# Saving matmuls by sevens in four more blocks, and one weight sum of each seven made by an accumulating transfer

## The chip, the cores and the metric

The kernel runs on 1 core of one Trainium2 chip. The metric is device time of one execution in microseconds (us). Of the kernel before there are three timed runs, with a median of 2232.99 us (2231.83 to 2235.12). Engines are called as in the profile: PE (TensorE, matmuls; PEld loads its weights), DVE (VectorE), ACT (ScalarE), POOL (GpSimd), SP (SyncE, which issues nearly all transfers).

## The reference, cut to what matters

Two layers on 256 tokens of width 2048. Each layer is a mixer (gated delta rule and gated linear recurrence in layer 0; two kinds of attention in layer 1) and then a SwiGLU feed-forward of inner width 5632; at the end stands an RMS norm over rows.

```python
h = h + mixer(rmsnorm(h, norm), ...)                 # w_in, w_out and the mixing between
h = h + swiglu(rmsnorm(h, ffn_norm[layer]), ffn_w_gate[layer], ffn_w_up[layer], ffn_w_down[layer])
...
def swiglu(hn, w_gate, w_up, w_down):
    return (jax.nn.silu(hn @ w_gate) * (hn @ w_up)) @ w_down
```

All is float32. The change touches the feed-forward, the first projection of the kernel and the last norm.

## The kernel before, in words

**A float32 product as three matmuls.** Every weight tile `raw` (128 x 1024 float32, 512 KB) is loaded by SP (L173 in `load`), rounded by ACT into a high half `whi` (L179) and subtracted by DVE into a low half `wlo` (L180). PE then adds x_high·w_high, x_high·w_low and x_low·w_high into a PSUM bank. In the feed-forward these are L404, L405 and L406 in `Bank.add`, with 512 columns each.

**Buffers.** `raw` has 3 buffers, and the feed-forward has 4 more (`raw4`): of each 7 loads 4 go to `raw4` and 3 to `raw`. `whi` has 4 buffers, `wlo` 3, `thi` and `tlo` 2 each. SP issues its loads in one order, each when a buffer is free.

**Blocks.** `ffn` (L482) walks over 11 pieces of the inner width, in three rounds of 4, 4 and 3. A round first makes each of its pieces with one block of gate and up weights (`in_gu`), and then has two down blocks (`in_dn`, p = 0 and 1), for two times 512 columns each. A `block` (L409) holds four result banks `F[t][i]`, for token half t and result i.

**Sevens.** A group m of four weight tiles (two rows of tiles by two results) costs 8 products with two token halves, 48 matmuls. Where m is in `comb`, `seven` (L424) does it by seven products, as in Winograd's form of Strassen's rule, 42 matmuls. It needs sums of weight tiles, made by `total` (L372): DVE adds (L375), ACT rounds (L378, `thi`), DVE subtracts (L379, `tlo`). The sums, of four tiles b11, b12, b22 and b21, are T1 = b11 + b12, T3 = b12 + b22, T2 = T1 + b22, T4 = T2 + b21 (the signs lie on the token side). It also needs sums of the token side, made by `combine` (L382 to L393) once for four tiles of x. The products go to four more banks M0 to M3, which `ends` (L449) folds into `e` tiles: one copy by ACT (L451) and four adds by DVE (L453). Gate and up blocks have two groups by sevens (the first has none), down blocks have one. The steps of the sevens are spread between the plain units of the block (L476); `hooks` places side work at a plain unit, such as `turn` (L487: transposes of the gated result through banks `Ph`) and `late` (L504: `combine` for the down blocks).

**Order.** The instructions of each engine are put in order when the kernel is built, by a scheduler with estimated costs; semaphores then hold them to their data. At the end of the second feed-forward the order of DVE and ACT is written by hand (`second_half`, L1137).

**Start and end.** `first` (L210) makes four projections from 16 tiles of x and weights, loaded as four single tiles and then pairs (L219); high and low halves are made tile by tile for the first two pairs and then pair by pair (L227). After each four tiles ACT squares them (L250). At the end, the row norm is taken from partial sums of squares `ssp` (L317); `root` (L1142) makes two small DVE steps (L1145) and a square root on ACT (L1147), `rate` inverts it (L1151 to L1153), `ready` scales and stores (L1157, L1159, L1161).

Of the kernel before, what the change touches and what calls it, by code (L numbers as in the profile page):

```python
# [5 lines left out]
AF = mybir.ActivationFunctionType  # L6
# [4 lines left out]
D = 2048  # L11
# [36 lines left out]
def body(tc, A, out):  # L48
# [161 lines left out]
    def first(src, n, w):  # L210

        m = T + n * 128
        xw = [h.rearrange("p a b -> p (a b)")] + [ogp.tile([128, 4 * D // 2], F32, name=f"xw{i}", tag="og") for i in range(3)]
        xw = [t[:, 0:4 * m].rearrange("p (k n) -> p k n", n=m) for t in xw]
        Ps = [acc.tile([128, T], F32, name="Pw", tag="acc") for _ in range(n)]
        for a, b in [(k, k + 1) for k in range(4)] + [(k, k + 2) for k in range(4, NK, 2)]:  # L219
            nc.sync.dma_start(xw[a // 4][:, a % 4:a % 4 + b - a], src[:, a:b])  # L220
            if b == 12:
                nc.sync.dma_start(tab[:, 0:NTAB0], A["tab"][:, 0:NTAB0])
                nc.sync.dma_start(col[:, 16:], A["col"][:, 16:])
        for u in range(NK // 2):
            hi = wh.tile([128, 1024], F32R, name="whi")
            lo = wl.tile([128, 1024], F32R, name="wlo")
            for a, b in [(0, 1), (1, 2)] if u < 2 else [(0, 2)]:  # L227
                ks = range(2 * u + a, 2 * u + b)
                for k in ks:
                    x = xw[k // 4][:, k % 4, 0:T]  # L230
                    S.activation(X[:, k, 0], x, AF.Copy, scale=w[:, k:k + 1])
                    V.scalar_tensor_tensor(out=X[:, k, 1], in0=x, scalar=w[:, k:k + 1], in1=X[:, k, 0].bitcast(F32),
                                           op0=ALU.mult, op1=ALU.subtract)
                raw = xw[u // 2][:, u % 2 * 2 + a:u % 2 * 2 + b, T:]
                c = slice(512 * a, 512 * b)
                rows = lambda t: t[:, c].rearrange("p (k n) -> p k n", n=n * 128)
                if u == a == 0:
                    V.tensor_copy(rows(hi), raw)
                else:
                    S.copy(rows(hi), raw)  # L240
                V.tensor_sub(rows(lo), raw, rows(hi).bitcast(F32))
                for k in ks:
                    for i, P in enumerate(Ps):
                        ws = slice((k % 2 * n + i) * 128, (k % 2 * n + i + 1) * 128)
                        PE.matmul(P, hi[:, ws], X[:, k, 0], start=k == 0, stop=False)
                        PE.matmul(P, hi[:, ws], X[:, k, 1], start=False, stop=False)
                        PE.matmul(P, lo[:, ws], X[:, k, 0], start=False, stop=k == NK - 1)
            if u % 2:
                sq = xw[u // 2][:, :, 0:T]
                tc.keep_in_program_order(S.activation(sq, sq, AF.Square))  # L250
        return Ps, [t[:, :, 0:T] for t in xw]
# [60 lines left out]

    def sumsq(g, *ts):
        for t in ts or range(2):
            j = (mx.tile([128, 1024], F32, name="junk", tag="T", bufs=3)[:, 0:512] if more else
                 mx.tile([128, 512], F32, name="junk", tag="t2", bufs=4))
            S.activation(j, h[:, t, g * 512:(g + 1) * 512], AF.Square, accum_out=ssp[:, t, g:g + 1])  # L317

# [50 lines left out]
        return f  # L369


    def total(a, b, name):  # L372

        t = mx.tile([128, 1024], F32, name=name, tag="T", bufs=3)
        V.tensor_tensor(out=t, in0=a, in1=b, op=ALU.add)  # L375
        hi = fp.tile([128, 1024], F32R, name="thi", tag="thi", bufs=2)
        lo = fp.tile([128, 1024], F32R, name="tlo", tag="tlo", bufs=2)
        S.copy(hi, t)  # L378
        V.tensor_sub(lo, t, hi.bitcast(F32))  # L379
        return t, (hi, lo)  # L380

    def combine(x4):  # L382

        f = mx.tile([128, 4, T], F32, name="cf", tag="T", bufs=3)
        c = mx.tile([128, 4, 2, 128], F32, name="cc4", tag="T", bufs=3)
        r = fp.tile([128, 2, 4, 2, 128], F32R, name="comb", tag="comb", bufs=3)
        V.tensor_tensor(out=f, in0=x4[:, :, 0].bitcast(F32), in1=x4[:, :, 1].bitcast(F32), op=ALU.add)
        a11, a21, a12, a22 = (f[:, 2 * j:2 * j + 2, t * 128:(t + 1) * 128] for j in range(2) for t in range(2))
        for i, (x, y) in enumerate(((a21, a22), (a21, a11), (a22, c[:, 1]), (a12, c[:, 2]))):
            V.tensor_tensor(out=c[:, i], in0=x, in1=y, op=ALU.subtract)  # L390
        S.copy(r[:, 0], c)
        V.tensor_tensor(out=r[:, 1], in0=c, in1=r[:, 0].bitcast(F32), op=ALU.subtract)
        return r  # L393

    class Bank:
# [3 lines left out]
        def add(self, A, B):  # L399

            hi, lo = (t.rearrange("p (k n) -> p k n", n=512) for t in B)
            for kk in range(2):
                xh, xl = A(kk)
                PE.matmul(self.t, xh, hi[:, kk], start=self.i == kk == 0, stop=False)  # L404
                PE.matmul(self.t, xh, lo[:, kk], start=False, stop=False)  # L405
                PE.matmul(self.t, xl, hi[:, kk], start=False, stop=kk == 1 and self.i == self.n - 1)  # L406
            self.i += 1

    def block(src, x, comb, nd, hooks, tail=0, lead=2, trail=None):  # L409

# [13 lines left out]
        def seven(m):  # L424
# [16 lines left out]
            M[2].add(cx(2), w)  # L441
            yield
            b21 = load(src(0, 2 * m + 1))
            F[0][0].add(q(1, 0), split(b21))
            yield
            F[1][0].add(q(1, 1), total(t, b21, "T4")[1])
            yield

        def ends():  # L449
            c1, v, w5, w7 = (mx.tile([128, 512], F32, name=f"e{i}", tag=f"e{i}", bufs=1) for i in range(4))  # L450
            S.copy(c1, M[0].t)  # L451
            for o, a, b, op in ((v, M[2], c1, ALU.subtract), (w5, M[1], v, ALU.add), (v, M[3], v, ALU.add), (w7, M[3], w5, ALU.add)):
                V.tensor_tensor(out=o, in0=a.t, in1=b, op=op)  # L453
# [28 lines left out]
    def ffn(L, then, fin=None):  # L482
# [18 lines left out]
        for groups in ((0, 2, 2, 2), (2, 2, 2, 2), (2, 2, 2)):  # L501
# [3 lines left out]
            for j in range(piece):  # L505
# [8 lines left out]
                a = [fp.tile([128, 512], F32, name=f"fa{t}", tag="fa", bufs=2) for t in range(2)]  # L514
                for t in range(2):
                    if e:
                        V.tensor_tensor(out=a[t], in0=F[t][0], in1=e[t][0], op=(ALU.add, ALU.subtract)[t])
                    S.activation(a[t], a[t] if e else F[t][0], AF.Silu, scale=nrm["rs"][:, t:t + 1])
                for t in range(2):
                    if e:  # L520
                        V.tensor_tensor(out=e[t][1], in0=F[t][1], in1=e[t][1], op=ALU.add)
                    V.scalar_tensor_tensor(out=a[t], in0=e[t][1] if e else F[t][1], scalar=nrm["rs"][:, t:t + 1], in1=a[t],
                                           op0=ALU.mult, op1=ALU.mult)
                    todo.append((hid, j, t, a[t]))
                b += 1
            u0 = 2 * (b - piece)
            for p in range(2):
                end = b == NB and p == 1
                hooks = {2: turn} if todo else {}
                if p == 0 and piece == 4:  # L530
                    hooks.update(late)
                if end and fin:
                    hooks.update({5: lambda: then(0), 6: lambda: then(1)})
                last = (3, 1, 3) if end and fin else (0, 5 if 4 in hooks else 2)
                F, e = block(lambda i, u: dn[2 * p + i, u0 + u], lambda k: hid[:, k], {0: lambda: ch[0]}, piece, hooks, *last)
                hs = [[h[:, t, (2 * p + i) * 512:(2 * p + i + 1) * 512] for i in range(2)] for t in range(2)]
                for t in range(2):
                    for i in range(2):
# [598 lines left out]
    def second_half(add):  # L1137

        o = fo[0]
        x, y, z = ([f[:, t:t + 1] for t in range(2)] for f in (xf, yf, zf))  # L1140

        def root(t):  # L1142

            for i, o in ((2, z[t]), (3, x[t])):
                V.scalar_tensor_tensor(out=o, in0=ssp[:, t, i:i + 1], scalar=1.0 / D, in1=part[:, t:t + 1] if i == 2 else z[t],  # L1145
                                       op0=ALU.mult, op1=ALU.add)
            S.activation(y[t], ssp[:, t, 3:4], AF.Sqrt, scale=1.0 / D, bias=z[t])  # L1147

        def rate(t):
# [15 lines left out]
        add(0, 1)  # L1165
        sumsq(3, 0)
        add(1, 0)
        root(0)
        sumsq(2, 1)
# [107 lines left out]
```

## Time and profile before

| | |
|---|---|
| median of 3 runs | 2232.99 us |
| the profiled execution | 2232.51 us, of which its span is 2230.7 us |
| granted PE clock | 0.999 |
| instructions on PE / DVE / ACT / POOL | 11026 / 2716 / 1670 / 6 |
| weights and other data moved | 422.29 MB, mean 189 GB/s |
| feed-forward of layer 0 and of layer 1 | about 424 to 1152 us and 1526 to 2221 us of the span |

A line of the page's list of groups gives source line, engine, operation, result and inputs, how many, then busy time and mean duration of one; behind the second bar stands the idle time of the engine just before them and what ended it. In a timeline, a row begins with its start and its duration in us. PE overlaps matmuls: one of 512 columns is shown with 0.39 us, though the next begins 0.23 us after it.

### The profile page before, as it was taken

The page shows a single profiled execution, that of the slowest core. Times are in us where ns is not written, and L with a number is a line of the kernel's source. Part 1 is how long each engine was busy: PE and PEld are TensorE (multiplying, and loading weights), DVE is VectorE, ACT ScalarE, POOL GpSimd, SP SyncE. Part 2 cuts the span into 40 slices and gives each one's busy share as a digit, 9 for nine tenths or more (in the row PEclk, how much of TensorE's full clock was granted, in tenths as well). Part 3 has the DMA queues.
Part 4 walks back from the last instruction along what each step waited for, and adds up shares of the span by engine and source line. Part 5 has one row for each costly group of instructions (what it writes and reads, how often), then busy time and mean ns, then how long its engine had stood idle before and what let it go on. Part 6 is the DMA issues. An engine that isn't in the chain of part 4 may idle for free.

```text
span 2230.7 us, 30096 instructions
## 1 busy us (share of the span) xinstructions
PE 2215.9 (99%) x11026; PEld 1852.0 (83%) x11026; DVE 1928.9 (86%) x2716; ACT 1278.9 (57%) x1670; POOL 2.1 (0%) x6
## 2 busy tenths in 40 slices
PE   9999999999999999999999999999999999999998
PEld 8888888888888888888878888888888888888886
DVE  8899676789989999899966658857999999999998
ACT  6776664565555665565654444445665466555565
POOL 0000000000000000000000000000000000000000
PEclk9999999999999999999999999999999999999999
DMA  7445445665565666656545455456665666666563
GB/s 280 161 144 168 140 150 187 214 208 195 192 215 196 201 195 203 207 187 200 180 158 175 158 172 172 162 186 217 208 198 191 208 205 203 194 210 202 181 219 131
DMA packets 117780, 422.29 MB, mean 189 GB/s; under 512 B 13152, under 2 KB 14688, under 8 KB 117504
## 3 DMA queue, kind: packets, MB, share of 16 engines
q1 hardware_dynamic: 117344, 420.10, 56.7%
q8 instruction: 86, 1.41, 0.2%
q14 instruction: 62, 0.51, 0.1%
q10 hardware_dynamic: 288, 0.27, 0.0%
HBM read 418.22 MB, written 2.10 MB: 188 GB/s over the span
## 4 chain that ended last, share of the span: by engine, by line
PE 97%; DVE 1%; DMA 1%; ACT 0%; issue 0%; SPq 0%; DVEq 0%; ACTq 0%
PE F L405 16%; PE F L406 16%; PE F L404 16%; PE Pw L199 11%; PE Pw L204 6%; PE Px L303 5%; PE Px L305 5%; PE Px L304 5%; PE M L404 4%; PE M L405 4%; PE M L406 4%; PE Ph L492 1%; PE Psc L1053 1%; PE Pt L326 0%; PE Ps L563 0%; DMA raw<-in_gu 0%
## 5 line engine op out<-in xcount | busy, mean ns | idle before, releaser
L179 ACT CAST whi<-raw 128x1024 fp32r<-128x1024 f32 x724 | 760.7, 1052 | 744.8 <-PE F L406 359.1
L180 DVE TENSOR_TENSOR wlo<-raw,whi 128x1024 fp32r<-128x1024 f32 x724 | 876.5, 1219 | 185.0 <-PE Px L304 74.0
L199 PE MATMUL Pw<-X,whi 128*128 128x512 f32 x1088 | 388.0, 400 | 0.0
L404 PE MATMUL F<-whi,X 128*128 128x512 f32 x848 | 330.5, 391 | 0.0
L405 PE MATMUL F<-wlo,X 128*128 128x512 f32 x848 | 330.4, 390 | 0.0
L406 PE MATMUL F<-whi,X 128*128 128x512 f32 x848 | 330.1, 389 | 0.0
L204 PE MATMUL Pw<-X,wlo 128*128 128x256 f32 x1088 | 304.7, 280 | 0.1
L378 ACT CAST thi<-T 128x1024 fp32r<-128x1024 f32 x208 | 219.1, 1054 | 98.6 <-DVE T L375 71.5
L379 DVE TENSOR_TENSOR tlo<-T,thi 128x1024 fp32r<-128x1024 f32 x208 | 252.5, 1219 | 24.7 <-ACT thi L378 24.2
L199 PEld LDWEIGHTS Pw<-X,whi 128*128 128x128 f32 x1088 | 204.1, 188 | 47.4 <-issue 0.5
L405 PE MATMUL F<-wlo,hid 128*128 128x512 f32 x536 | 208.9, 390 | 0.0
L406 PE MATMUL F<-whi,hid 128*128 128x512 f32 x536 | 208.7, 389 | 0.0
L404 PE MATMUL F<-whi,hid 128*128 128x512 f32 x536 | 208.6, 390 | 0.0
L204 PEld LDWEIGHTS Pw<-X,wlo 128*128 128x128 f32 x1088 | 205.4, 189 | 1.2 <-DVE wlo L180 0.7
L406 PEld LDWEIGHTS F<-whi,X 128*128 128x128 f32 x848 | 159.2, 188 | 33.1
L404 PEld LDWEIGHTS F<-whi,X 128*128 128x128 f32 x848 | 159.2, 188 | 32.7
L405 PEld LDWEIGHTS F<-wlo,X 128*128 128x128 f32 x848 | 159.3, 188 | 32.5
L375 DVE TENSOR_TENSOR T<-raw,raw 128x1024 f32<-128x1024 f32 x98 | 119.2, 1218 | 11.0 <-DMA raw<-in_gu 8.9
L375 DVE TENSOR_TENSOR T<-T,raw 128x1024 f32<-128x1024 f32 x104 | 126.6, 1218 | 1.9 <-DMA raw<-in_dn 1.7
L404 PE MATMUL M<-thi,comb 128*128 128x512 f32 x312 | 121.3, 391 | 0.6 <-ACT thi L378 0.6
L405 PE MATMUL M<-tlo,comb 128*128 128x512 f32 x312 | 121.6, 390 | 0.0
L406 PE MATMUL M<-thi,comb 128*128 128x512 f32 x312 | 121.5, 389 | 0.0
(385 smaller groups left out, 3217.1 us busy)
## 6 DMA issues: line engine op xcount, KB each, us to landing
raw<-in_gu SPq DMA_DIRECT2D x352, 512.0 KB, 4.1
raw<-in_dn SPq DMA_DIRECT2D x176, 512.0 KB, 4.3
raw<-in_w0w SPq DMA_DIRECT2D x72, 512.0 KB, 3.6
raw<-in_wo SPq DMA_DIRECT2D x64, 512.0 KB, 3.5
raw<-in_w1w SPq DMA_DIRECT2D x64, 512.0 KB, 3.6
raw<-in_w1x SPq DMA_DIRECT2D x32, 512.0 KB, 3.6
raw<-in_w0x SPq DMA_DIRECT2D x16, 512.0 KB, 3.6
xw<-in_xw SPq DMA_DIRECT2D x6, 768.0 KB, 10.9
```

The source lines that it names most:

```text
L179: S.copy(hi, raw)
L180: V.tensor_sub(lo, raw, hi.bitcast(F32))
L199: PE.matmul(P.rearrange("p a b -> p (a b)"), hi[:, kk], X[:, k].rearrange("p a b -> p (a b)"), start=k == 0, stop=False)
L204: PE.matmul(P[:, 0], lo[:, kk], X[:, k, 0], start=False, stop=k == NK - 1)
L303: PE.matmul(Ps[t], x[:, 0, ts], hi[:, kk], start=k == 0, stop=False)
L304: PE.matmul(Ps[t], x[:, 0, ts], lo[:, kk], start=False, stop=False)
L375: V.tensor_tensor(out=t, in0=a, in1=b, op=ALU.add)
L378: S.copy(hi, t)
L379: V.tensor_sub(lo, t, hi.bitcast(F32))
L404: PE.matmul(self.t, xh, hi[:, kk], start=self.i == kk == 0, stop=False)
L405: PE.matmul(self.t, xh, lo[:, kk], start=False, stop=False)
L406: PE.matmul(self.t, xl, hi[:, kk], start=False, stop=kk == 1 and self.i == self.n - 1)
```

## The change

1. **One sum by a transfer.** As soon as DVE has made T1, POOL issues a transfer that loads the tile of b22 a second time and adds it to b12 in place, so that b12's buffer comes to hold T3. DVE's add for T3 is gone. T3's product (into M3) is moved from fourth to last of the seven; its high and low halves are made by a new function `halves`.
2. **Two groups by sevens in two down blocks per layer**: p = 1 of the rounds of 4, in place of one. Their second `combine` is hooked to the down block before.
3. **Fewer buffers.** T1, T2 and T4 share one buffer; the tag `T` goes from 3 to 2 buffers; `comb` goes from 3 to 4.
4. **The gate in place of the bank sums**: `fa` is gone, its values are kept in the `e` tiles.
5. **Round of 3**: its `combine` for the down blocks moves from plain unit 4 to 6.
6. **First loads**: six single tiles, and three pairs handled tile by tile. **End**: the two small steps of `root` become `mean`, placed separately.

```diff
-        for a, b in [(k, k + 1) for k in range(4)] + [(k, k + 2) for k in range(4, NK, 2)]:
+        for a, b in [(k, k + 1) for k in range(6)] + [(k, k + 2) for k in range(6, NK, 2)]:
...
-            for a, b in [(0, 1), (1, 2)] if u < 2 else [(0, 2)]:
+            for a, b in [(0, 1), (1, 2)] if u < 3 else [(0, 2)]:
...
+    def halves(t):
+        hi = fp.tile([128, 1024], F32R, name="thi", tag="thi", bufs=2)
+        lo = fp.tile([128, 1024], F32R, name="tlo", tag="tlo", bufs=2)
+        S.copy(hi, t)
+        V.tensor_sub(lo, t, hi.bitcast(F32))
+        return hi, lo
...
             b12 = load(src(1, 2 * m))
-            t, w = total(b11, b12, "T1")
+            t, w = total(b11, b12)
+            G.dma_start(b12, src(1, 2 * m + 1), accum_op=ALU.add)
             M[1].add(cx(0), w)
             yield
             b22 = load(src(1, 2 * m + 1))
             F[0][1].add(cx(3), split(b22))
             yield
-            M[3].add(cx(1), total(b12, b22, "T3")[1])
-            yield
-            t, w = total(t, b22, "T2")
+            t, w = total(t, b22, t)
             M[2].add(cx(2), w)
...
-            F[1][0].add(q(1, 1), total(t, b21, "T4")[1])
+            F[1][0].add(q(1, 1), total(t, b21, t)[1])
+            yield
+            M[3].add(cx(1), halves(b12))
             yield
...
-                    hooks.update(late)
+                    hooks[6] = late[4]
...
+                    hooks[9] = lambda hid=hid: ch.update({1: combine(hid[:, 4:8])})
...
-                F, e = block(lambda i, u: dn[2 * p + i, u0 + u], lambda k: hid[:, k], {0: lambda: ch[0]}, piece, hooks, *last)
+                F, e = block(lambda i, u: dn[2 * p + i, u0 + u], lambda k: hid[:, k],
+                             {m: lambda m=m: ch[m] for m in range(1 + (p == 1 and piece == 4))}, piece, hooks, *last)
...
+        def mean(t, i):
+            V.scalar_tensor_tensor(out=(z, x)[i][t], in0=ssp[:, t, 2 + i:3 + i], scalar=1.0 / D,
+                                   in1=z[t] if i else part[:, t:t + 1], op0=ALU.mult, op1=ALU.add)
...
         add(1, 1)
         sumsq(3, 1)
+        mean(1, 0)
         ready(0, 2)
         ready(0, 3)
         root(1)
+        mean(1, 1)
```

More of the change, by code (lines that the diff above doesn't have):

```diff
@@ L314, in sumsq @@
         for t in ts or range(2):
-            j = (mx.tile([128, 1024], F32, name="junk", tag="T", bufs=3)[:, 0:512] if more else
+            j = (mx.tile([128, 1024], F32, name="junk", tag="T", bufs=2)[:, 0:512] if more else
                  mx.tile([128, 512], F32, name="junk", tag="t2", bufs=4))
@@ L369, in norm_then @@
         return f
-    def total(a, b, name):
-        t = mx.tile([128, 1024], F32, name=name, tag="T", bufs=3)
-        V.tensor_tensor(out=t, in0=a, in1=b, op=ALU.add)
+    def halves(t):
         hi = fp.tile([128, 1024], F32R, name="thi", tag="thi", bufs=2)
@@ L407, in add, with sums @@
             self.i += 1
+    def sums():
+        return [[mx.tile([128, 512], F32, name=f"e{t}{i}", tag=f"e{t}{i}", bufs=1) for i in range(2)] for t in range(2)]
     def block(src, x, comb, nd, hooks, tail=0, lead=2, trail=None):
@@ L445, in seven @@
             yield
-            F[1][0].add(q(1, 1), total(t, b21, "T4")[1])
+            F[1][0].add(q(1, 1), total(t, b21, t)[1])
+            yield
+            M[3].add(cx(1), halves(b12))
             yield
         def ends():
-            c1, v, w5, w7 = (mx.tile([128, 512], F32, name=f"e{i}", tag=f"e{i}", bufs=1) for i in range(4))
+            (c1, w5), (v, w7) = sums()
             S.copy(c1, M[0].t)
@@ L1167, in second_half @@
         add(1, 0)
+        mean(0, 0)
         root(0)
+        mean(0, 1)
         sumsq(2, 1)
```

29 lines of the change are left out of this document (15 added, 14 removed).

## The prediction

> **What bounds the kernel now.** I read first the page's list of engines and its chain that ended last, then the waits of PE, then PE's timeline inside the feed-forward.
>
> ```profile
> PE 2215.9 (99%) x11026; PEld 1852.0 (83%) x11026; DVE 1928.9 (86%) x2716; ACT 1278.9 (57%) x1670; POOL 2.1 (0%) x6
> ...
> PE 97%; DVE 1%; DMA 1%; ACT 0%; issue 0%; SPq 0%; DVEq 0%; ACTq 0%
> ```
>
> ```profile
> PE Pz L93 <- ACT tab L90: 2.7, 1, 2.7
> PE Pw L245 <- ACT whi L240: 0.7, 1, 0.7
> PE Pgate L645 <- ACT cx L582: 0.6, 1, 0.6
> PE M L404 <- ACT thi L378: 0.6, 1, 0.6
> PE F L405 <- DVE tlo L379: 0.4, 1, 0.4
> ```
>
> ```profile
> 742.77 0.39 PE L404 MATMUL F<-whi,X 128*128 128x512 f32 x1
> ...
> 748.21 0.39 PE L404 MATMUL M<-whi,X 128*128 128x512 f32 x1
> ```
>
> PE is the whole story: the chain runs through it for 97%, and its waits in 2230.7 us are five, 5.0 us in all, of which 1.0 us lies in the feed-forward (L404, L405). So no transfer and no other engine costs time there now, and what shortens the kernel is fewer matmuls, or less time before the first and after the last. The third fence gives the price: from the first row to the last are 24 matmuls in 5.44 us, 0.227 us each (the 0.39 of a row overlaps its successor).
>
> The nearest bound behind PE is DVE. In the two feed-forwards:
>
> ```profile
> core 0: us, PE busy (x) PEld busy (x) DVE busy (x) ACT busy (x) POOL busy (x), PEclk, DMA share, GB/s
> 424.00:1152.00 728.00, 727.60 (x3273) 601.47 (x3272) 679.81 (x739) 421.31 (x471) 0.00 (x0) 1.00 0.60 198
> 1526.00:2221.00 695.00, 694.33 (x3102) 573.15 (x3100) 655.35 (x698) 400.50 (x430) 0.00 (x0) 1.00 0.60 198
> ```
>
> DVE has 48 and 40 us to spare there, 6 to 7%; the transfer engines have 40%; ACT is far off.
>
> **The change part by part.** The sum is made against the profiled execution, 2232.51 us (span 2230.7 and 1.8 around it); the median of the three runs lies 0.5 us above it.
>
> *Matmuls.* A group by sevens takes 42 matmuls in place of 48. Two blocks in each of two layers get one group more: 4 x 6 = 24 fewer, 24 x 0.227 = **-5.4 us**, all on the chain. No other edit takes or adds a matmul.
>
> *DVE's work.*
>
> ```profile
> L180 DVE TENSOR_TENSOR wlo<-raw,whi 128x1024 fp32r<-128x1024 f32 x724 | 876.5, 1219 | 185.0 <-PE Px L304 74.0
> L378 ACT CAST thi<-T 128x1024 fp32r<-128x1024 f32 x208 | 219.1, 1054 | 98.6 <-DVE T L375 71.5
> L379 DVE TENSOR_TENSOR tlo<-T,thi 128x1024 fp32r<-128x1024 f32 x208 | 252.5, 1219 | 24.7 <-ACT thi L378 24.2
> ...
> L375 DVE TENSOR_TENSOR T<-raw,raw 128x1024 f32<-128x1024 f32 x98 | 119.2, 1218 | 11.0 <-DMA raw<-in_gu 8.9
> L375 DVE TENSOR_TENSOR T<-T,raw 128x1024 f32<-128x1024 f32 x104 | 126.6, 1218 | 1.9 <-DMA raw<-in_dn 1.7
> ```
>
> ```profile
> L453 DVE TENSOR_TENSOR e<-M,e 128x512 f32<-128x512 f32 x128 | 84.8, 683 | 1.7 <-PE M L406 1.4
> ...
> L390 DVE TENSOR_TENSOR cc<-cf,cc 128x256 f32<-128x256 f32 x20 | 8.3, 417 | 0.0
> ```
>
> There are 52 sevens now (208 sums by four) and 56 after. Adds fall from 208 to 3 x 56 = 168, -40 x 1.22 = -48.7 us. The four new sevens bring 16 `tlo` (+19.5) and take 4 `wlo` (-4.9). Four more `combine` cost each two rows of 1024 at 1.22 and four of 256 at 0.42: 4 x 4.1 = +16.4. Net -18 us of DVE, and ACT gains 16 `thi` at 1.05, less 4 `whi`, and 4 `combine` roundings: +17 us on an engine with 300 us free per layer. A gate block with two sevens goes from 30 DVE rows of 1024 to 28 (6 adds, 8 `tlo`, 14 `wlo`); heavier are only p = 1 of the rounds of 4, from 23 to the same 28, and p = 0 by one `combine`. PE's time in a block with two sevens is 180 matmuls, 40.8 us; DVE's is 28 x 1.14 = 31.9 (rows back to back, quoted below) and twelve rows of 512 (0.68 each, about 0.62 apart by the same overlap), 39.3 together. So I cost all this at **0**, hidden by PE; without that cover a block would pay what DVE exceeds PE by.
>
> *The transfer that adds.* The trace has no transfer issued by POOL and none that adds. The nearest rows are plain loads of the same 512 KB, and the slowest landing of any load is that of the crowded start:
>
> ```profile
> raw<-in_gu SPq DMA_DIRECT2D x352, 512.0 KB, 4.1
> ...
> tab<-in_tab SPq DMA_DIRECT2D x1, 140.0 KB, 11.2
> ```
>
> From below: 4.1 us; from above: 11.2. I take 8.2, two plain loads, since the old bytes have to be fetched as well as the new; it is nearer to the same size in the same stage. What that may cost depends on when the sum is wanted. In the built order of the changed kernel, DVE has between its T1 add and the last reading of that buffer 12 rows of 1024 and one of 512 in the tightest case; back to back such rows begin 1.14 us apart:
>
> ```profile
> 745.24 1.22 DVE L379 TENSOR_TENSOR tlo<-T,thi 128x1024 fp32r<-128x1024 f32 x1
> ...
> 748.65 1.22 DVE L180 TENSOR_TENSOR wlo<-raw,whi 128x1024 fp32r<-128x1024 f32 x1
> ```
>
> (3.41 us for three). So at least 14 us, on average 20, less 1.1 for ACT's rounding: at least 13 us for 4.1 to 11.2. It is behind nothing on POOL, whose own work is 2.1 us. Cost **0**. [...]
>
> In bytes, 56 x 0.52 = 29 MB more on 422; if each counts double, the share of 0.60 in the windows goes to some 0.72.
>
> *Buffers.* This is what the change pays with. b12's buffer is now held from the T1 add to the end of the seven, on average 20 us of DVE rows in that order, where it was 5. That is one of seven buffers, for most of the time. SP's waits show that loads are already released by buffers:
>
> ```profile
> SPq L173 <- DVE wlo L180: 1425.7, 571, 6.8
> SPq L173 <- DVE T L375: 287.6, 139, 6.4
> ```
>
> Counting DVE rows from the release of a load to its first use, in each built order, the median over the feed-forwards' 528 loads falls from 15.5 to 13.9 us, and loads with 6 to 12 us go from 66 to 162; but those under 6, where a landing of 4.1 could be late, fall from 56 to 32. Cost taken: **0**, from -1.0 (the two feed-forward waits go) to +5 (as in the first rival).
>
> *Bank sums in place, fewer `T`, `late` moved.* No row is added. M3 filled last asks for its bank later, which is easier on `turn`, whose transposes share these banks. **0**, both ways under 0.5.
>
> *Start.*
>
> ```profile
> 8.63 0.60 ACT L240 CAST whi<-h 128x512 fp32r<-128x512 f32 x1
> 9.27 1.06 ACT L250 ACTIVATE h<-h 128x1024 f32<-128x1024 f32 x1
> 10.24 0.89 ACT L231 ACTIVATE X<-xw,col 128x256 fp32r<-128x256 f32 x2
> 11.04 1.03 ACT L240 CAST whi<-xw 128x1024 fp32r<-128x1024 f32 x1
> ```
>
> ```profile
> 11.19 0.28 PE L247 MATMUL Pw<-X,wlo 128*128 128x256 f32 x1
> 12.12 0.38 PE L245 MATMUL Pw<-X,whi 128*128 128x256 f32 x1 [0.65 <-ACT whi L240]
> ...
> 13.05 0.28 PE L246 MATMUL Pw<-X,whi 128*128 128x256 f32 x1
> 13.38 0.74 PE L247 MATMUL Pw<-X,wlo 128*128 128x256 f32 x4
> ```
>
> PE's matmuls here begin 0.12 us apart, so it loses 0.81 before 12.12 and 0.21 before 13.38. ACT is busy with the squares until 10.24 either way; after that one tile's x row (half of 0.89) and its half-width rounding (0.60, as in the first row) let PE begin at 11.3 in place of 12.12, and its low half is ready as early. I take **-0.8** (between 0, if the sixth tile's row is then late by as much, and -1.0).
>
> *End.*
>
> ```profile
> 2221.77 1.41 DVE L1159 SCALAR_TENSOR_TENSOR fin<-h,fin,fin 128x512 f32<-128x512 f32 x2
> 2223.09 0.42 DVE L1145 SCALAR_TENSOR_TENSOR fin<-ssp,fin 128x1 f32<-128x1 f32 x2
> 2223.67 0.16 DVE L1151 RECIPROCAL fin<-fin 128x1 f32<-128x1 f32 x1 [0.15 <-ACT fin L1147]
> ```
>
> ACT's root waits for the small steps behind two scalings. After, it needs only the one ahead of them, and runs beside them; DVE goes from the scalings to one small step to the reciprocal, at about 2223.4 in place of 2223.67. **-0.3** (0 to -0.4).
>
> Sum: -5.4 - 0.8 - 0.3 = -6.5; 2232.5 - 6.5 = **2226.0 us**, -0.3%.
>
> **Rivals.**
>
> 1. *Loads come late after all* (buffers held, adding transfers beside them). For it: the 162 loads at 6 to 12 us, which leave less room for a landing that has doubled. Against it: DVE gets lighter, and ACT waits mostly for PE. Price: if one in ten of the 162 is late by 0.3 us on PE, 5 us: 2231.
> 2. *The sums land after their readers.* ACT takes its work in order, so a late sum holds every rounding behind it, and PE runs dry: this decides from a landing of some 13 us. At 18 us, 11 of the 28 sums of a layer would be late by 24 us together; with half of it covered by tiles that PE has in stock, 2 x 12 = +24: 2250 us, slower. For it: no row has an adding transfer. Against it: nothing in the trace lands later than 11.2.
> 3. *DVE and POOL get in each other's way.* If preparing a transfer held DVE for one row (1.22 us), 56 x 1.22 = 68 us: that would still fit into 18 saved and 88 spare on average, but not where the sevens are. A block with two of them has 39.3 + 2.4 = 41.7 us of DVE against PE's 40.8; 24 such blocks x 0.9 = +20, DVE having no room to run ahead: 2246 us, slower. It decides from 0.75 us per transfer. The other order (DVE holding POOL back) ends in rival 2. [...]
> 4. *The change doesn't do what it says*: PE keeps its pace but what it gains at the start is lost at the next wait. Then -5.4 alone, 2227.1; it lies in the forecast's range.
>
> **How the numbers follow.** Forecast 0.70 (with rival 4), its own range 2223.5 to 2228.3: DVE lighter may take the two feed-forward waits and some short ones with it. Rival 1 0.14 (2228 to 2234), rival 2 0.09, rival 3 0.07. The range leaves out rivals 2 and 3: 2223.0 to 2231.5. A measurement of this kernel tells about 0.2%, 4.5 us, from no change. Faster by over that: 0.70 and a quarter of rival 1, 0.74; within it 0.10; slower 0.16.
>
> **What would show it.** Right: PE has 24 matmuls fewer, no PE wait over 1 us in the feed-forwards, DVE busy some 18 us less, the first matmul of the fifth tile near 11.3 us, a tail behind the last matmul that is 0.3 us shorter. The adding transfers land under 13 us, and neither ACT nor DVE waits for them. Wrong: ACT rows of `thi` that wait for a transfer (rival 2); PE waits for `whi` behind loads (rival 1); DVE rows of 1024 longer than 1.22 us where POOL issues (rival 3).

## The result, and the profile after

The changed kernel takes **2225.39 us** (median of 7 runs, 2224.23 to 2228.40) where the kernel before, measured beside it, takes 2233.59 (2231.83 to 2235.62): ratio 0.9964 (in brackets, here and below, its 95% interval: [0.9955, 0.9974]), 8.2 us less. Measured a second time (experiment e1) the ratio is 0.9977 [0.9968, 0.9987], 5.6 us less. The forecast was 2226.0 us, 6.5 less, and lies between the two.

The profiled execution of the changed kernel took 2228.4 us (span 2226.6), the longest of its seven; the sums below are made against its own span, 4.1 us shorter than the 2230.7 of before. First the page of the changed kernel: its engines and its chain that ended last.

```profile
PE 2211.8 (99%) x11002; PEld 1847.0 (83%) x11002; DVE 1917.1 (86%) x2713; ACT 1284.9 (58%) x1687; POOL 50.6 (2%) x62
...
PE 95%; DVE 2%; issue 1%; ACT 1%; DMA 1%; DVEq 0%; ACTq 0%
```

PE has 24 matmuls fewer (11026 before) and is still the whole story. Its waits:

```profile
PE Pz L93 <- ACT tab L90: 2.7, 1, 2.7
PE M L410 <- DVE tlo L377: 1.0, 2, 0.8
PE Pw L204 <- DVE wlo L180: 0.9, 1, 0.9
PE Pgate L660 <- ACT cx L597: 0.6, 1, 0.6
```

In the feed-forwards there is one group of waits (L410, 1.0 us); the wait in L204 is new and lies at 75 us, in the first mixer. The same two stretches that the prediction showed of before, from the view of windows (columns: stretch, its length, busy time and instructions of PE, PEld, DVE, ACT and POOL, granted clock, DMA share, GB/s):

```profile
424.00:1152.00 728.00, 727.16 (x3267) 600.11 (x3267) 674.61 (x739) 425.35 (x480) 24.32 (x28) 1.00 0.74 222
1526.00:2221.00 695.00, 691.57 (x3089) 570.36 (x3087) 648.28 (x698) 405.40 (x444) 24.17 (x28) 1.00 0.72 217
```

DVE is less busy (679.81 and 655.35 before), POOL carries 28 transfers in each, and the DMA share is 0.74 and 0.72 instead of 0.60 (0.72 was estimated). Where the time went is read from PE's timeline: the first and the last matmul of each feed-forward, here the four rows of the changed kernel.

```profile
432.41 0.39 PE L409 MATMUL F<-whi,X 128*128 128x512 f32 x1
...
1127.87 0.39 PE L411 MATMUL F<-whi,hid 128*128 128x512 f32 x1
...
1524.55 0.39 PE L409 MATMUL F<-whi,X 128*128 128x512 f32 x1
...
2217.49 0.39 PE L411 MATMUL F<-whi,hid 128*128 128x512 f32 x1
```

The same rows of before and of e1 give this table (us; a stretch runs from the start of its first matmul to the start of its last):

| stretch | before | after | e1, the same kernel again |
|---|---|---|---|
| start to first feed-forward | 430.95 | 432.41 (+1.46) | 432.15 (+1.20) |
| feed-forward 0 | 697.13 | 695.46 (-1.67) | 694.54 (-2.59) |
| between | 396.63 | 396.68 | 396.68 |
| feed-forward 1 | 696.03 | 692.94 (-3.09) | 692.78 (-3.25) |
| behind the last matmul | 9.99 | 9.13 (-0.86) | 9.13 (-0.86) |
| span | 2230.72 | 2226.62 | 2225.28 |

So the gain lies in the two feed-forwards (-4.8 and -5.8) and at the end; the start is longer in both executions, though it was edited to be shorter.

### The profile page after: what moved, and what is told of

It is laid out like the page before. It is cut to its first block, busy times and chain, and to the rows that moved or that the text cites. A ratio compares the mean times of both kernels' runs of the same rounds, so it can differ in the third digit from the quotient of the medians.

```text
span 2226.6 us, 30372 instructions
## 1 busy us (share of the span) xinstructions
PE 2211.8 (99%) x11002; PEld 1847.0 (83%) x11002; DVE 1917.1 (86%) x2713; ACT 1284.9 (58%) x1687; POOL 50.6 (2%) x62
## 3 DMA queue, kind: packets, MB, share of 16 engines
q0 software_dynamic: 8064, 29.36, 7.8%
## 4 chain that ended last, share of the span: by engine, by line
PE 95%; DVE 2%; issue 1%; ACT 1%; DMA 1%; DVEq 0%; ACTq 0%
PE F L411 15%; PE F L410 15%; PE F L409 15%; PE Pw L199 10%; PE Pw L204 5%; PE Px L303 5%; PE Px L304 5%; PE Px L305 5%; PE M L410 5%; PE M L411 4%; PE M L409 4%; PE Ph L503 1%; DVE wlo L180 1%; PE Psc L1068 1%; PE Pt L326 0%
## 5 line engine op out<-in xcount | busy, mean ns | idle before, releaser
L410 PE MATMUL F<-wlo,X 128*128 128x512 f32 x848 | 330.4, 390 | 0.0
L204 PE MATMUL Pw<-X,wlo 128*128 128x256 f32 x1088 | 304.8, 280 | 1.0 <-DVE wlo L180 0.9
L376 ACT CAST thi<-T 128x1024 fp32r<-128x1024 f32 x168 | 176.6, 1051 | 124.1 <-DVE T L384 84.0
L377 DVE TENSOR_TENSOR tlo<-T,thi 128x1024 fp32r<-128x1024 f32 x168 | 205.1, 1221 | 28.0 <-ACT thi L376 27.3
L204 PEld LDWEIGHTS Pw<-X,wlo 128*128 128x128 f32 x1088 | 205.3, 189 | 2.4 <-DVE wlo L180 2.0
L409 PE MATMUL F<-whi,hid 128*128 128x512 f32 x480 | 187.5, 391 | 0.0
L411 PE MATMUL F<-whi,hid 128*128 128x512 f32 x480 | 186.9, 389 | 0.0
L410 PE MATMUL F<-wlo,hid 128*128 128x512 f32 x480 | 186.8, 389 | 0.0
L410 PEld LDWEIGHTS F<-wlo,X 128*128 128x128 f32 x848 | 159.2, 188 | 32.4
L384 DVE TENSOR_TENSOR T<-T,raw 128x1024 f32<-128x1024 f32 x112 | 136.5, 1219 | 1.1 <-DMA raw<-in_gu 0.2
L410 PE MATMUL M<-tlo,comb 128*128 128x512 f32 x336 | 131.8, 392 | 1.1 <-DVE tlo L377 1.0
L409 PE MATMUL M<-thi,comb 128*128 128x512 f32 x336 | 131.4, 391 | 0.0
L411 PE MATMUL M<-thi,comb 128*128 128x512 f32 x336 | 130.9, 390 | 0.0
L411 PEld LDWEIGHTS F<-whi,hid 128*128 128x128 f32 x480 | 90.1, 188 | 18.8
```

The source lines that it names most:

```text
L204: PE.matmul(P[:, 0], lo[:, kk], X[:, k, 0], start=False, stop=k == NK - 1)
```

## The experiments

**The theory**: what is gained is 24 matmuls, nothing else of the sum is needed for the time, and the adding transfer costs nothing because it is done long before its reader and DVE is relieved by it. **The rivals**: (a) loads come late behind buffers and transfers, (b) the sums land too late, (c) DVE had room anyway and the transfer does no work, (d) start and end carry the gain. All kernels are compared with the kernel before on the same chip. "Feed-forwards" is the sum of both stretches of the table above, in the profiled execution of each kernel.

| kernel | sevens | sum T3 by | median, us | ratio | feed-forwards |
|---|---|---|---|---|---|
| before | 52 | DVE | 2233.4 to 2233.8 | 1 | 1393.2 |
| changed | 56 | transfer | 2225.39 | 0.9964 [0.9955, 0.9974] | 1388.4 |
| e1 changed, again | 56 | transfer | 2228.19 | 0.9977 [0.9968, 0.9987] | 1387.3 |
| e2 | 56 | DVE | 2242.05 | 1.0035 [1.0022, 1.0048] | 1403.9 |
| e3 | 52 | transfer | 2245.53 | 1.0056 [1.0043, 1.0070] | 1405.7 |
| e4 old start and end | 56 | transfer | 2227.82 | 0.9974 [0.9963, 0.9985] | 1388.1 |
| e5 e2, combine at hook 4 | 56 | DVE | 2244.72 | 1.0049 [1.0037, 1.0062] | 1405.1 |
| e6 e3, eight load buffers | 52 | transfer | 2232.92 | 0.9998 [0.9989, 1.0007] | 1392.9 |
| e7 two transfers per sum | 56 | two transfers | 2247.27 | 1.0067 [1.0054, 1.0079] | 1405.9 |
| e8 old start, new end | 56 | transfer | 2227.88 | 0.9975 [0.9966, 0.9984] | 1388.3 |
| e9 neither part | 52 | DVE | 2239.11 | 1.0025 [1.0016, 1.0034] | 1399.9 |
| e10 transfer that doesn't add | 56 | (overwritten) | 2227.52 | 0.9975 [0.9965, 0.9986] | 1388.0 |
| e11 combine at hook 4 | 56 | transfer | 2228.15 | 0.9976 [0.9966, 0.9986] | 1388.4 |

**e1**, the changed kernel unaltered.

> The changed kernel once more, unchanged, for a second profile. If its gain over the kernel before is 24 matmuls and the two ends, 2225 to 2226.5 us again, and about 8 us under the kernel before. The profiled execution of the first run was 3 us above its median, with one PE wait of 0.9 us at 75 us of the span and a longer slow clock at the start; if these are chance, the second profile lacks the wait and its first real matmuls speed up earlier. If they come from the changed first loads, they are there again.

Measured: 2228.19 us (2226.71 to 2229.92), above the 2225 to 2226.5 that were expected; PE's wait at 75 us is there again (1.2 us). The interval overlaps that of the first measurement; e4, e8 and e11, whose edits turn out not to matter, give 2227.8 to 2228.2 as well. About -5.6 us is therefore the better supported size; why the first seven runs lay 2.8 us lower is open.

**e2**, DVE adds b22 into b12 in place of the transfer:

```diff
-            G.dma_start(b12, src(1, 2 * m + 1), accum_op=ALU.add)
...
             F[0][1].add(cx(3), split(b22))
             yield
+            V.tensor_tensor(out=b12, in0=b12, in1=b22, op=ALU.add)
```

> DVE adds b22 to b12 in place, behind the load of b22; no transfer adds. All else as changed: M3 last, 56 sevens. 56 rows of 1.22 us go back to DVE, a gate block has 30 rows again. Theory (PE bounds, DVE's rows are covered): 2225 to 2229 us, PE waits in the feed-forwards under 3 us. Rival (DVE has become the bound where the sevens are dense, and the transfer buys the gain): 2232 us or more, with PE waits for tlo or wlo of 6 us or more.

Measured: 2242.05 us, 13.9 above e1. The list of PE's waits names DVE; then the timeline of DVE up to the end of the first of them, and the windows ahead of, in and behind it:

```profile
PE F L410 <- DVE wlo L180: 6.2, 2, 3.1
```

```profile
1021.11 0.69 DVE L533 TENSOR_TENSOR e<-F,e 128x512 f32<-128x512 f32 x1 [0.26 <-PE F L411]
1021.71 1.22 DVE L397 TENSOR_TENSOR comb<-cc,comb 128x1024 fp32r<-128x1024 f32 x1
1022.85 1.41 DVE L534 SCALAR_TENSOR_TENSOR e<-e,rs,e 128x512 f32<-128x512 f32 x2
1024.17 3.49 DVE L180 TENSOR_TENSOR wlo<-raw,whi 128x1024 fp32r<-128x1024 f32 x3
```

```profile
960.00:1022.00 62.00, 61.79 (x274) 49.87 (x272) 60.74 (x66) 36.51 (x41) 0.00 (x0) 1.00 0.62 197
1022.00:1026.00 4.00, 0.91 (x2) 0.54 (x3) 4.00 (x5) 0.78 (x1) 0.00 (x0) 0.81 0.00 0
1026.00:1032.00 6.00, 6.00 (x17) 4.66 (x16) 4.02 (x4) 1.84 (x2) 0.00 (x0) 0.56 0.81 246
```

DVE has been busy for 60.74 of 62 us and comes to the `wlo` that PE wants (1024.17) only after bank sums, `combine` and gate, 3 us late. A busy DVE alone doesn't make the wait: in the kernel before it is as busy in the same stretch (this row), and PE loses nothing.

```profile
960.00:1022.00 62.00, 62.00 (x278) 50.98 (x277) 60.77 (x66) 37.79 (x40) 0.00 (x0) 1.00 0.58 189
```

What differs is how late DVE comes to the tile. In the 6 us behind the wait PE makes 17 matmuls instead of 26, at a granted clock of 0.56. Counted from matmul to matmul, the two waits with what follows them cost 6.2 and 5.1 us. That explains the feed-forwards for the most part: 1393.2 - 5.4 + 11.3 = 1399.1 of 1403.9 (the other 4.8: e9). Rival (c) falls: with 56 sevens DVE has no room for the fourth add in this block.

**e3**, the transfer kept, 52 sevens:

```diff
-                    hooks[9] = lambda hid=hid: ch.update({1: combine(hid[:, 4:8])})
...
-                             {m: lambda m=m: ch[m] for m in range(1 + (p == 1 and piece == 4))}, piece, hooks, *last)
+                             {m: lambda m=m: ch[m] for m in range(1)}, piece, hooks, *last)
```

> The four added groups by sevens are taken back (52 sevens, all with the adding transfer). Theory: 24 matmuls at 0.227 us come back, 5.4 us: 2230 to 2231.5. Rival (the lighter DVE shortened the feed-forwards by itself): 2225 to 2228.

Measured: 2245.53 us, 17.3 above e1, a miss by some 14 us. PE's waits; ACT's timeline ahead of the first of them, at 702.44 us; DMA issues between 696 and 704.4 us with their median time to landing; and PE's timeline:

```profile
PE M L409 <- ACT thi L376: 7.9, 2, 4.2
```

```profile
696.07 1.06 ACT L179 CAST whi<-raw 128x1024 fp32r<-128x1024 f32 x1 [0.30 <-PE F L411]
704.43 1.04 ACT L179 CAST whi<-raw 128x1024 fp32r<-128x1024 f32 x1 [7.31 <-DMA raw<-in_gu]
705.39 1.04 ACT L376 CAST thi<-raw 128x1024 fp32r<-128x1024 f32 x1
```

```profile
raw<-in_gu SPq DMA_DIRECT2D x3, 512.0 KB, 7.0
raw<-in_gu POOLq DMA_DIRECT2D x1, 512.0 KB, 8.7
```

```profile
702.44 0.39 PE L411 MATMUL F<-thi,X 128*128 128x512 f32 x1
706.48 0.50 PE L409 MATMUL M<-thi,comb 128*128 128x512 f32 x1 [3.65 <-ACT thi L376]
707.74 0.80 PE L410 MATMUL M<-tlo,comb 128*128 128x512 f32 x1 [0.76 <-DVE tlo L377]
708.33 0.63 PE L411 MATMUL M<-thi,comb 128*128 128x512 f32 x1
...
710.89 0.46 PE L411 MATMUL F<-whi,X 128*128 128x512 f32 x1
711.20 0.40 PE L409 MATMUL F<-whi,X 128*128 128x512 f32 x1
```

SP's load of 696.1 us was issued 0.6 us behind an adding transfer and landed 8.2 us later, 704.3, where loads of this kernel take 4.4 in the median. ACT stood 7.31 us for it, and the rounding of an earlier sum, complete since 682.5 us, stood behind it in ACT's order. PE, from 702.44 to 711.20, made ten matmuls in 8.76 us instead of 2.27: 6.5 us lost, of which the waits are 4.4. The same happens at 1802 us (8.1 us lost by the same count). This is the prediction's first rival, in a kernel whose source differs from the changed one only by the four sevens; its built order differs in places behind them, from some 612 us on, and here too.

**e4**, start and end as before:

```diff
-        for a, b in [(k, k + 1) for k in range(6)] + [(k, k + 2) for k in range(6, NK, 2)]:
+        for a, b in [(k, k + 1) for k in range(4)] + [(k, k + 2) for k in range(4, NK, 2)]:
...
-            for a, b in [(0, 1), (1, 2)] if u < 3 else [(0, 2)]:
+            for a, b in [(0, 1), (1, 2)] if u < 2 else [(0, 2)]:
...
         def root(t):
+            for i, o in ((2, z[t]), (3, x[t])):
+                V.scalar_tensor_tensor(out=o, in0=ssp[:, t, i:i + 1], scalar=1.0 / D, in1=part[:, t:t + 1] if i == 2 else z[t],
+                                       op0=ALU.mult, op1=ALU.add)
```

(and the four calls of `mean` are gone).

> First loads, their handling and the end's small steps as in the kernel before; the rest as changed. Theory: 0.8 us at the start and 0.3 at the end come back: 2226 to 2227. Rival (the ends gave nothing, the profile of the changed kernel being no earlier at 56 us of the span): 2225.4, no difference.

Measured: 2227.82 us, 0.4 below e1: no difference that this measurement can tell. The predicted 1.1 us is not seen, though intervals of 0.1% (2 us) to either side don't exclude it. That start and end carry the gain (rival d) falls. The feed-forwards take 1388.1, the same as with the new start and end.

**e5**, e2 with the `combine` of the rounds of three back at hook 4:

```diff
-                    hooks[6] = late[4]
+                    hooks.update(late)
```

> As e2 (no adding transfer, VectorE adds b22 into b12), but the combine of the rounds of three is again at hook 4 together with the rest of `late`, as in the kernel before. Theory A (in e2 VectorE was short only around that combine; the two PE waits of 3.1 us and the slow matmuls behind them, 6.5 us each, are all that e2 lost): the waits go, 2242 - 13 = about 2229 us. Theory B (VectorE is short wherever two sevens stand in a block, so the waits turn up elsewhere): 2238 us or more, with PE waits on wlo or tlo of over 2 us.

Measured: 2244.72 us. The list of PE's waits still has `wlo`, at 1025 and 2126 us:

```profile
PE F L410 <- DVE wlo L180: 3.9, 2, 2.0
```

Theory A fell: moving the `combine` turns two waits of 3.1 into two of 2.0 with three gaps of 0.6 to 0.9 us between PE's matmuls ahead of each; counted from matmul to matmul the two places cost 6.3 and 5.4 us, as in e2, and the time stays. Without the transfer DVE is short in that block wherever the `combine` stands.

**e6**, e3 with eight load buffers:

```diff
-        if more and loads[0] > 0 and loads[0] % 7 in (1, 3, 5, 6):
-            raw = mx.tile([128, 1024], F32, name="raw4", tag="raw4", bufs=4)
+        if more and loads[0] > 0 and loads[0] % 8 in (1, 3, 5, 6, 7):
+            raw = mx.tile([128, 1024], F32, name="raw4", tag="raw4", bufs=5)
...
-        r = fp.tile([128, 2, 4, 2, 128], F32R, name="comb", tag="comb", bufs=4)
+        r = fp.tile([128, 2, 4, 2, 128], F32R, name="comb", tag="comb", bufs=3)
```

> As e3 (52 sevens, transfer kept), with eight load buffers in place of seven (the room comes from the fourth comb buffer, which 52 sevens do not need). Theory A (e3's two PE waits of 4 us come from a load that was released too late for a landing of 8.2 us, because b12 holds one of seven buffers): an eighth buffer releases each load some 3 us earlier, the waits and the half-speed matmuls behind them go, 2245.5 - 16 = about 2230 us. Theory B (the adding transfer beside a load makes it late whatever the buffers): 2240 us or more, with the same waits of PE on thi or whi.

Measured: 2232.92 us, 12.6 below e3 (about 2230 was expected); the waits on `thi` are gone. The longest PE waits of the page are now

```profile
PE Pz L93 <- ACT tab L90: 2.7, 1, 2.7
PE Pgate L659 <- ACT cx L596: 0.6, 1, 0.6
PE Pw L204 <- DVE wlo L180: 0.4, 1, 0.4
```

Loads have not become quicker: 65 of the feed-forwards' 528 take over 6 us (35 in e3), and yet PE no longer stands still for them. So e3's loss took two things, a slow landing and too few buffers to issue the load earlier. And e6 is the change without its four sevens and without e3's accident, but with an eighth buffer: ratio 0.9998 [0.9989, 1.0007], feed-forwards 1392.9 against 1393.2 before. Transfer, sums in place, start and end give nothing there without the sevens; the four sevens are the gain (1392.9 - 1388.1 = 4.8 us, the mean of the changed kernel, e1, e4, e8 and e11 being 1388.1). The eighth buffer does not enter when those five are set against the kernel before: 1393.2 - 1388.1 = 5.1 us, where 24 matmuls are 5.4.

**e7**, the transfer issued twice for each sum (the line `G.dma_start(..., accum_op=ALU.add)` stands there twice).

> The changed kernel with the adding transfer issued twice for each sum, so that M3 gets b12 + 2 b22 in place of b12 + b22 (that part of the output changes). The sum is complete some 14 us after the T add instead of 7. By the prediction's second rival (decides at a landing of 13 us, with an average of 20 us to the reader) about a fifth of the 56 sums are late by 1 to 3 us: 2232 to 2245 us, and ACT rows of thi wait for a DMA. If there is more room than that, or if the scheduler's stock of tiles covers it: 2226 to 2229 us, with no PE wait over 1 us. If it is the loads beside the transfers that count, PE waits for whi: over 2235 us with loads of over 8 us.

Measured: 2247.27 us, 19 above e1 and 2 above the range expected for late sums. PE's waits, and the group of ACT's roundings of the summed tiles (last columns: ACT's idle time before them and what ended most of it):

```profile
PE M L409 <- ACT thi L376: 11.1, 7, 2.5
PE M L410 <- DVE tlo L377: 2.3, 4, 1.4
```

```profile
L376 ACT CAST thi<-raw 128x1024 fp32r<-128x1024 f32 x56 | 58.8, 1050 | 29.0 <-PE M L411 13.2 <-DMA raw<-in_gu 12.8 <-DMA raw<-in_dn 2.0
```

and the same group in the changed kernel:

```profile
L376 ACT CAST thi<-raw 128x1024 fp32r<-128x1024 f32 x56 | 58.8, 1051 | 15.2 <-PE M L411 14.9 <-ACT whi L179 0.2
```

With one transfer ACT never waits for a sum; with two, it waits 14.8 us for them and PE loses 18 us in the feed-forwards. The room can be read from the rows: in the changed kernel ACT's rounding of a sum begins 13.0 us (at least) and 19.0 us (median) after the end of the T1 add, and never less than 4.4 us after the sum has landed. In e7 the second transfer begins when the first has landed, and the sums are complete 12.0 (at least) and 15.9 us (median) after that add. The second rival's mechanism is shown, at the room that the prediction counted in the built order (13 us and 20).

**e8**, the new end with the old start (the first two pairs of lines of e4's diff).

> The changed kernel with the start of the kernel before. Theory A (what the new start gains before 56 us is lost at PE's wait at 74.7 us, the new end gives 0.3 to 0.9 us): that wait is absent, the first feed-forward begins at about 433.5 us of the span instead of 434.1 to 434.3, and the time is 0.5 to 1.0 us below that of the changed kernel, 2227.2 to 2227.7 us by the same chip as e1. Theory B (the start's gain stays): 0.8 us above the changed kernel.

Measured: 2227.88 us, 0.3 below e1, so that theory B (0.8 above) isn't seen either. Theory A fell: the wait near 75 us is there, 1.6 us, with the old start. What it follows is the landing of one load of the first mixer, issued at 50.4 to 52.0 us. ACT's rounding of that tile, in the changed kernel and in e2 (same start):

```profile
56.95 1.06 ACT L179 CAST whi<-raw 128x1024 fp32r<-128x1024 f32 x1 [1.96 <-DMA raw<-in_w0w]
```

```profile
55.65 1.05 ACT L179 CAST whi<-raw 128x1024 fp32r<-128x1024 f32 x1 [0.70 <-DMA raw<-in_w0w]
```

| that load's landing, us | PE's wait near 75 us |
|---|---|
| 4.4 (e4), 4.5 (before, e2), 4.8 (e3) | none |
| 5.0 (e11), 5.3 (e6), 5.5 (e9) | 0.2, 0.4, 0.8 |
| 5.8 (changed), 6.0 (e1, e10) | 0.9, 1.2, 1.3 |
| 6.1 (e8), 6.2 (e5), 6.4 (e7) | 1.6, 1.2, 1.6 |

The wait goes with the landing, in kernels with the old start (e4, e8, before) and the new. So of the +1.46 and +1.20 us ahead of the first feed-forward 0.9 and 1.2 are this wait, and not the start's edit.

**e9**, e5 with 52 sevens (e3's diff): neither the transfer nor the additional sevens.

> As e5 (VectorE adds, combine at hook 4), but with 52 sevens: neither the transfer nor the additional sevens, the other edits kept (sums in place, two T buffers, M3 last, start, end). Theory A (VectorE had room for four adds in each of 52 sevens, and it is the sevens added in the down blocks that take its lead, so that the gate block at 1025 us finds it late): e5's two PE waits go, and the time is the kernel before's, 2231 to 2235 us. Theory B (the sums in place with two T buffers, or M3 last, are what stalls the gate block): the waits stay, 2240 us or more.

Measured: 2239.11 us, between the two theories. The waits of 2 us went from the list of PE's waits, as theory A said:

```profile
PE Pz L93 <- ACT tab L90: 2.7, 1, 2.7
PE M L409 <- ACT thi L376: 0.9, 3, 0.4
PE M L410 <- DVE tlo L377: 0.8, 2, 0.6
```

but the feed-forwards take 6.7 us more than before; thirteen gaps of 0.2 to 0.8 us between PE's matmuls hold 4.6 of them. The edits that are left (two `T` buffers, sums in place, M3 last with b12's buffer held until then) therefore cost some 5 to 7 us where DVE does the adds. Where the transfer does them no such cost is seen: the changed kernel's feed-forwards lie within 0.3 us of 1393.2 - 5.4. Which of these edits it is was not tried.

**e10**, a transfer that overwrites (`accum_op=ALU.add` left out).

> The changed kernel with the GpSimd transfer not adding: it overwrites b12 with b22, so that M3 gets b22 alone (that part of the output changes); bytes, buffers, order and queue are the same. Theory A (the adding makes the transfer long, since the old bytes are fetched too, and it is what slows the loads beside it): it lands in 4 to 5 us instead of 7.0, and loads of over 6 us fall from some 45 to 15 or fewer. Theory B (it is GpSimd's queue or its descriptors): 6.5 to 7.5 us as before. The time is 2225 to 2229 us in both cases, since nothing waits for the sums.

Measured: 2227.52 us. The transfers' landing, in e10 and in the changed kernel:

```profile
DMA to landing us min/median/max: 3.8/4.6/9.0
```

```profile
DMA to landing us min/median/max: 5.2/7.0/9.4
```

Theory A: the adding is what takes time. Loads over 6 us fall from 44 to 19, a little more than the 15 expected. The time is the same, as nothing waits for either.

**e11**, the changed kernel with e5's edit alone.

> The changed kernel with the combine of the rounds of three at hook 4 together with the rest of `late`, as in the kernel before: that one edit undone. The prediction's cost of it is 0: 2227.5 to 2229 us. Theory against it (VectorE is at its limit in that block, as e2 and e5 show without the transfer): two PE waits of 1 to 2 us near 1025 and 2125 us with slow matmuls behind them, 2231 to 2237 us.

Measured: 2228.15 us, as e1. With the transfer the place of this `combine` costs nothing, as predicted.

## Why the prediction was right, and where it was not

**The sum.** The forecast, 6.5 us less, lies between the two measurements, but only the sevens' 5.4 and the end's 0.3 came about much as written; the 0.8 of the start did not last. That the sum fits all the same is partly luck: 0.8 is less than the 2.8 us by which the two measurements of the same kernel differ, for a reason that is not known.

**Bounds.** Right. PE stayed at 99%, and no transfer or other engine took its place.

**Matmuls, -5.4.** Right, and the whole of the gain: 24 matmuls fewer, -4.8 and -5.8 us in two executions of the feed-forwards, and 4.8 between e6 and the changed kernels.

**DVE's work, at nothing.** Right in the sum, too easy in its reason. The rows' durations fell by 16.8 us (18 predicted), DVE's busy time by 11.8, as fewer rows overlap. But "48 and 40 us to spare" is an average, and says little. The prediction counted a gate block with two sevens, 39.3 us of DVE against PE's 40.8, and not the one that also carries a `combine` (4.1): with eight adds that is 30 x 1.14 + 7.4 + 4.1 = 45.7 us, with six 43.4. Such a block can only be passed on a lead that DVE has from blocks ahead. The kernel before and e9 pass it without a long wait; with the four sevens ahead of it and the adds on DVE (e2, e5) it costs 11 us. That the lead is used up there follows from these four runs; the lead itself was not measured. So the transfer is not needed for 52 sevens, nor would DVE's average have forbidden the other four; it is what makes them affordable, which the prediction did not see.

**The adding transfer, 8.2 us (4.1 to 11.2).** Right: 7.0 in the median, 9.4 at most, and 0.86 us of POOL each. The reason given for 8.2, that the old bytes are fetched as well as the new, is not shown: the queue q0 counts 29.36 MB with the adding and without (e10). What is shown is the time, 7.0 us against 4.6. No one waits for it, and e7 shows where the room ends, some 13 us for the tightest sums; its loss, 18 us with the sums complete at 15.9, is also of the size that rival 2 gave (24 at 18). The bound of 11.2 was misread: the list of issues has the median of each group, and single loads at the crowded start of the kernel before took up to 12.9 us (`xw`, 768 KB), close to rival 2's 13. "Nothing in the trace lands later than 11.2" is therefore not so; in the feed-forwards before no load took over 7.3.

**Buffers, at nothing (to +5).** Right for this kernel, by less than the text suggests. 44 of its 528 feed-forward loads take over 6 us, 7 of 528 before. PE loses nothing by it here, but in e3 two such landings cost 14 us, three times the upper bound: the estimate counted many small delays (16 x 0.3), and what came was two large ones, with half as much again behind them at a lower clock (0.62 granted from 708 to 712 us). The rival's chance, 0.14, was fair; its price was too small. Why this order escapes and e3's doesn't is settled only so far: with one buffer more e3 escapes too, and a slow landing alone isn't enough, as the changed kernel's load of 700.71 us, also issued 0.6 us behind an adding transfer, took 8.9 us and PE has no wait between 695 and 725 us. The changed kernel with eight buffers was not tried.

**Bank sums in place, T, `late`.** `late`: nothing, shown by e11. The others were not undone beside the transfer; e9 shows that they are not free without it.

**Start, -0.8.** The step was right at its place and failed behind it. The stall of 0.81 us ahead of the fifth tile is gone; the 150th matmul behind the fifth tile's first starts at 30.47 (changed) and 30.15 (e1) against 30.85 (before), 31.24 (e4) and 31.26 (e8), some 0.8 us earlier on the mean. (Over all executions the mean is 30.27 for ten with the new start and 31.12 for three with the old.) "The fifth tile near 11.3" failed in this execution: it was 12.13, because PE began at 5.15 instead of 4.74 and its matmuls stood 0.21 us apart until 7.67 (5.96 before), and 0.12 behind it. The trace's record of the granted clock begins, with 1.00, at 7.75 (5.92 before); where it begins varies from execution to execution, from 5.9 to 7.6 with the old start and from 6.3 to 9.2 with the new; e6, with the new start and 6.3, has its fifth tile at 11.30. By the first feed-forward it can't be seen any more: of the executions without a wait at 75 us, the old start reaches it at 430.95 and 431.62, the new at 431.05 and 431.13. That is rival 4's outcome; where on the way the lead is lost was not followed.

**End, -0.3 (0 to -0.4).** The mechanism was right, the size too small: 9.13 us behind the last matmul instead of 9.99. DVE's timeline at the end of the changed kernel:

```profile
2218.53 0.15 DVE L1159 SCALAR_TENSOR_TENSOR fin<-ssp,fin 128x1 f32<-128x1 f32 x1
2218.59 1.41 DVE L1176 SCALAR_TENSOR_TENSOR fin<-h,fin,fin 128x512 f32<-128x512 f32 x2
2219.92 0.15 DVE L1159 SCALAR_TENSOR_TENSOR fin<-ssp,fin 128x1 f32<-128x1 f32 x1
2220.17 0.16 DVE L1168 RECIPROCAL fin<-fin 128x1 f32<-128x1 f32 x1
```

The reciprocal starts 2.68 us after the last matmul's start, 2.93 before (2223.67 - 2220.74): that is the 0.3 of the prediction. The remaining 0.6 lies behind it and varies: e4, with the old end, has 9.43 in all; of eleven executions with the new, ten have 9.06 to 9.17, and e3 9.66. Set against e4 the new end gains 0.3.

**Rival 3** didn't come: DVE's rows of 1024 take 1.219 us as before, beside 56 transfers from POOL. From the costliest groups of the changed kernel:

```profile
L180 DVE TENSOR_TENSOR wlo<-raw,whi 128x1024 fp32r<-128x1024 f32 x720 | 874.5, 1219 | 189.3 <-PE Px L304 70.1
```

That preparing a transfer would hold DVE was an assumption, and no row shows it.

## What to carry to other kernels

On a kernel bound by PE, count the matmuls for the gain and the other engines block by block for whether you get it: the spare time of an engine over a stage says nothing of the one block that has two jobs more. Moving an add from DVE into a transfer pays by making room in that block, and costs a buffer for as long as the sum waits, and slower landings for the loads beside it (5.2 us in the median against 4.3); here the distance to the reader was 13 us or more for landings of up to 9.4, and two transfers one after the other (e7, sums complete 15.9 us behind the T1 add in the median) were too much; a buffer to spare was what saved e6. A PE wait can cost more than its length: 3.1 us cost 6.2 and 5.1 in e2, and 4.4 us cost 6.5 in e3.

## What the runs showed of the hardware

- **A wait can halve PE's clock behind it.** Matmuls of 512 columns start 0.227 us apart, and 0.427 apart for 6 to 12 of them behind the longer waits of e2, e3, e5 and e7. The granted clock is 0.50 there for 3.4 us (e2 from 2126.95, e3 from 707.62, e5 from 2128.86, e7 from 959.88) or 6.8 us (e2 from 1024.44, e3 from 1806.71, e5 from 1026.35). The windows ahead of, in and behind e3's first wait:

```profile
702.00:706.00 4.00, 0.83 (x4) 0.37 (x2) 0.00 (x0) 1.56 (x2) 0.00 (x0) 1.00 0.80 303
706.00:708.00 2.00, 0.76 (x2) 0.45 (x3) 1.54 (x2) 2.00 (x3) 0.00 (x0) 0.91 0.03 10
708.00:712.00 4.00, 4.00 (x12) 3.15 (x13) 3.18 (x3) 1.00 (x2) 0.00 (x0) 0.62 0.45 131
712.00:716.00 4.00, 4.00 (x20) 3.27 (x19) 2.75 (x3) 2.59 (x4) 0.00 (x0) 1.00 0.57 160
```

  Counting from one matmul's start to the next, it followed all six gaps of 2.46 to 4.62 us in e2, e3 and e5 (the 2.46 of e5 with three gaps of 0.6 to 0.9 ahead of it), but of e7's gaps of 2.08, 2.44, 2.61 and 2.86 us only that of 2.61, which stood alone; no shorter gap that stood alone in a feed-forward was followed by it. Why the gap of 2.86 was not is not shown.
- **An adding transfer takes about twice a plain one's time on the DMA engines, and slows loads beside it.** From the page of the changed kernel, the queues with packets, MB and share of the 16 engines:

```profile
q1 hardware_dynamic: 117488, 420.10, 58.3%
q0 software_dynamic: 8064, 29.36, 7.8%
```

  Per MB that is 0.27% against 0.14%. It is the adding and not the queue: in e10 the same queue moves the same bytes without adding for 4.1%.

```profile
q0 software_dynamic: 8064, 29.36, 4.1%
```

  In the changed kernel the 315 feed-forward loads with no adding transfer beside them land in 4.3 us in the median and 7.2 at most, the 121 with one beside them for 2 us or more in 5.2 and 9.0. The 23 that SP issues within 1 us behind one land in 6.9 in the median; behind e10's transfers it is 5.4.
- **One load's landing can move the kernel by over a microsecond.** The load at 51 us took 4.4 to 6.4 us from execution to execution, and PE waited up to 1.6 us some 25 us later, not at all where it took 4.8 us or less.
